# FFN of a decoder block by seven products: sums of products on top of copies in PSUM, last transposes between half pieces, and one weight-block sum by accumulating DMA

## The chip, the cores and the metric

The kernel runs on one core of one Trainium2 chip. The metric is the device time of one execution in microseconds, lower is better; the median of several executions is what two kernels are compared by. Beside the time there is one profiled execution, from which all rows below are read.

## What is computed

The reference is a whole decoder block for 512 tokens of width 2048 in float32: two attention branches merged by gates, then a SwiGLU FFN with 5632 hidden columns. The change touches the FFN alone:

```python
h2 = _rms(x, g_norm2) * (1 + sc2) + sh2
gate, up = jnp.split(h2 @ w_ffn_in, 2, axis=-1)
x = x + gt2 * ((jax.nn.silu(gate) * up) @ w_ffn_out)
```

Here `sh2`, `sc2` and `gt2` are vectors of 2048 that are computed from a conditioning vector.

## The kernel before

**The products.** Each of the two FFN matrix products is cut into 2 x 2 blocks and done with seven block products in place of eight (Strassen's scheme in Winograd's form). The blocks of a weight matrix are called 11, 21, 12, 22; the blocks of the activations are 11, 12, 22 and the sums "1" to "4" (S1 to S4). `PROD` says what each product multiplies: P1 takes weight block 11, P5 the difference 12 - 11, P7 the difference of 22 and that, P3 block 22, P6 the difference of 22 and 11, P2 block 21, P4 the difference of 21 and 22's running sum. So four of the seven products (P5, P7, P6, P4) need a sum of two weight blocks, made by VectorE (DVE) in the buffer of one of them (`piece_make`; `INTO` names that buffer and `LAST` says which buffers a product frees).

**A piece.** Every float32 product is done in three passes with a high and a low part of each operand (`mm3`). A weight piece is a tile of 128 x 1024, 512 KB: loaded by SP's DMA queue into one of ten buffers `raw`, cast to its high part `whi` by ScalarE (ACT), the rest `wlo` made by DVE, then used by 12 TensorE matmuls of 128 x 512. There are three `whi` and three `wlo` buffers. `ahead_to(i, 2, 6)` sets the order: before piece i is used, pieces up to i+2 are made and up to i+6 are loaded. All engines run their instructions in the order in which this walk emits them, each engine its own list.

**Stage a** (`ffn_in_group`, `w_ffn_in`) has 11 groups of hidden columns; each product of a group is four pieces. The first four groups are "early": their P1 and P2 are made ahead in one stretch (32 pieces) and parked in DRAM, so their group loop has P5, P7, P3, P6, P4 only. The others run P1, P5, P7, P3, P6, P2, P4. Products accumulate in four pairs of PSUM banks: A (tags s, s), B (t, t), C (mm, mm), D (mm, y). Partial results that several outputs share are evacuated and added by DVE (`p1`, `z`, `u`, `c12`; tiles of 128 x 512); after P4 a silu and a product by `z` follow. `act_back1` and `act_back2` transpose the two hidden halves back on TensorE (4 transposes into a bank of tag mm, 4 into one of tag y), split them into high and low parts and park them in DRAM by GpSimd's (POOL) queue; `act_back2` also makes the sums S1 to S4. `act_back2` of a group runs in the next group: after P1, or in early groups after P5. That of group 10 runs behind P1 of stage b.

**Stage b** (`ffn_out_chunk`, `w_ffn_out`) goes through five chunks of groups and the two halves q = 0 and 1 of the output columns; parked activations (`yb`) come back by SP's queue. After each product DVE adds its bank to an accumulator `acc`; in the final chunk `finish` combines them after P6, and `out_tiles` transposes the results on TensorE, adds them to the residual `xo` by DVE and stores them. The end of the program is the final chunk for q = 0 and then for q = 1, in the order P1, P5, P7, P3, P6, P2, P4.

In the rows, line L83 is that of a helper which records every operation, so tiles are told apart by names; L179 issues SP's DMAs, L1370 and L1400 the parks, L1545 the stores of the output.

Of the kernel before, what the change touches and what calls it, by code (L numbers as in the profile page):

```python
# [88 lines left out]
def kernel(  # L89
# [943 lines left out]

    def half_cols(th):
        return slice(th * 256, th * 256 + 256)
# [36 lines left out]
    X = {}  # L1072

    def norm2(k, th):
# [6 lines left out]
        if name != (2, 1):  # L1081
# [3 lines left out]
            X[name, k % 8] = x[:, 0:256], x[:, 256:512]  # L1085
        act.activation(t, t, AF.Identity, bias=sh)

    def sums(a, b, put):
# [7 lines left out]
        vec.tensor_tensor(s34[:, hi], b[:, lo], s12[:, hi], ALU.subtract)  # L1096
# [42 lines left out]
    BLOCK = {"11": (0, 0), "21": (1, 0), "12": (0, 1), "22": (1, 1)}  # L1139
# [21 lines left out]

    def kmc(key, ap):
# [12 lines left out]
    INTO = {"P5": "11", "P7": "12", "P6": "22", "P4": "21"}  # L1175
    LAST = {"P7": ("12",), "P6": ("11",), "P4": ("21", "22"), "E1": ("11",), "E2": ("21",)}

    def piece_keys(stage, g, prod, j):
        _, x, y = PROD[prod]
        return [(stage, g, b, j) for b in (y, x) if b]  # L1180

    def piece_make(stage, g, prod, j):
        _, x, y = PROD[prod]
        key = (stage, g, x, j)
        if y:
            kd = (stage, g, INTO[prod], j)
            vec.tensor_tensor(raws[kd], raws[key], raws[stage, g, y, j], ALU.subtract)
            key = kd
# [6 lines left out]
        for b in LAST.get(prod, ()):  # L1195
            del raws[stage, g, b, j]
# [4 lines left out]
    cur = {"load": 0, "make": 0}  # L1201
# [6 lines left out]
    def add_do(fn):  # L1208
        ev.append((None, fn))

    def ahead_to(i, n_make, n_load):
        while cur["load"] < min(i + n_load + 1, len(pieces)) or cur["make"] < min(i + n_make + 1, len(pieces)):
# [4 lines left out]
            else:  # L1217
                made[cur["make"]] = piece_make(*pieces[cur["make"]])
# [13 lines left out]
    def prod_mm(bank, hl, w, kk, first, last):  # L1232
# [3 lines left out]
        xh, xl = hl  # L1236
# [31 lines left out]
    def ffn_in_group(g, early):  # L1268
# [21 lines left out]
        def copy_to(name, bank):  # L1290
            def fn(t):
                G[name, t] = t2(name)
                act.copy(G[name, t], G[bank][t])
            both(fn)

        def add_bank(name, bank, out=None):
            def fn(t):
                dst = G[name, t] if out is None else t2(out)
                vec.tensor_tensor(dst, G[name, t], G[bank][t], ALU.add)
                G[out or name, t] = dst  # L1300
            both(fn)

        def after_p6(t):
            u, z = G["u", t], G["z", t]
            vec.tensor_tensor(z, z, u, ALU.add)
# [342 lines left out]
```

## Time and profile before

| | us |
|---|---|
| median of 3 runs | 2665.55 |
| lowest and highest | 2661.05, 2666.24 |
| profiled execution | 2668.23 |
| its span, first to last instruction | 2666.5 |
| stage a, ahead part and groups, about | 1308 to 2203 |
| stage b | 2203 to 2663 |

The profile lists the busy time of the engines: PE is TensorE's matmul, PEld its weight loads, DVE VectorE, ACT ScalarE, POOL GpSimd, SP the engine that issues most DMAs. A view by windows gives the same for stretches of the span, together with the granted TensorE clock (1.00 is full) and the share of the 16 DMA engines' time that is used. A view of waits names, for the idle time of an engine, what ended it.

### The profile page before, as it was taken

What the parts mean: (1) busy time and instruction counts of PE and PEld (TensorE: products, weight loads), DVE (VectorE), ACT (ScalarE), POOL (GpSimd) and SP (SyncE); (2) the same over time, 40 slices, a digit from 0 to 9 for tenths busy, and PEclk for the clock granted to TensorE, in tenths of its full rate; (3) what the DMA queues carried; (4) which work ended last, traced back from release to release, by engine and by line L of the source; (5) the groups of instructions that cost most, each with busy time, mean ns of one, the idle gap of its engine ahead of it and who ended that gap; (6) DMA issues with size and microseconds to landing.
All of it is one profiled execution on the core that took longest, in us unless ns stands there. A gap on an engine that the chain in (4) does not pass through costs nothing.

```text
span 2666.5 us, 32303 instructions
## 1 busy us (share of the span) xinstructions
PE 2582.4 (97%) x12166; PEld 2145.6 (80%) x12166; DVE 2023.5 (76%) x2622; ACT 1147.9 (43%) x1557; POOL 162.9 (6%) x270
## 2 busy tenths in 40 slices
PE   6999999999999999999899999999999999999998
PEld 4788888888998888888787777888878787888876
DVE  8967766656788764633688999888888887789997
ACT  4434655542333322322474545445554445533332
POOL 0000000000100100000000111011110011000000
PEclk9999999999999999999999999999999999999998
DMA  8854444336667694343575665554544459676561
GB/s 343 295 204 153 159 151 138 136 117 255 237 253 259 240 352 166 133 151 118 147 223 162 213 216 186 165 162 132 174 153 126 160 169 318 203 235 207 188 214 41
DMA packets 260901, 510.37 MB, mean 191 GB/s; under 512 B 16453, under 2 KB 181061, under 8 KB 235657
## 3 DMA queue, kind: packets, MB, share of 16 engines
q1 hardware_dynamic: 239136, 447.01, 49.4%
q0 software_dynamic: 15552, 50.61, 5.2%
q10 hardware_dynamic: 6056, 10.70, 1.1%
q8 instruction: 95, 1.56, 0.2%
q14 instruction: 62, 0.50, 0.1%
HBM read 445.86 MB, written 62.39 MB: 191 GB/s over the span
## 4 chain that ended last, share of the span: by engine, by line
PE 74%; issue 15%; DVE 6%; DMA 3%; POOL 1%; ACT 1%; SPq 0%; POOLq 0%; ACTq 0%; DVEq 0%
PE ps_mm L83 47%; PE ps_s L83 11%; PE ps_t L83 10%; PE ps_y L83 5%; DVE wlo L83 2%; DMA raw<-in_w_ff_dram 1%; DVE raw L272 1%; POOL apark L1370 1%; ACT whi L83 1%; DVE acc L83 1%; DVE raw L83 1%; DMA gpark<-sg 0%; DMA raw<-in_w_ada_dram 0%; DVE s L83 0%; DMA apark<-y34h 0%
## 5 line engine op out<-in xcount | busy, mean ns | idle before, releaser
L83 ACT CAST whi<-raw 128x1024 fp32r<-128x1024 f32 x672 | 703.0, 1050 | 1023.8 <-PE ps_mm L83 456.6
L83 DVE TENSOR_TENSOR wlo<-raw,whi 128x1024 fp32r<-128x1024 f32 x672 | 816.3, 1219 | 315.8 <-ACT whi L83 305.3
L83 DVE TENSOR_TENSOR raw<-raw,raw 128x1024 f32<-128x1024 f32 x264 | 319.1, 1221 | 28.0 <-DMA raw<-in_w_ff_dram 25.4
L83 PE MATMUL ps_mm<-hl,whi 128*128 128x512 f32 x832 | 327.6, 394 | 0.0
L83 PE MATMUL ps_mm<-hh,whi 128*128 128x512 f32 x832 | 325.5, 391 | 0.0
L83 PE MATMUL ps_mm<-hh,wlo 128*128 128x512 f32 x832 | 325.3, 391 | 0.0
L272 DVE CUSTOM_DVE_ANT_0 raw<-raw,cb,cols 128x2048 f32<-128x2048 f32 x96 | 224.6, 2345 | 1.0 <-DMA raw<-in_w_ada_dram 1.0
L83 PEld LDWEIGHTS ps_mm<-hh,wlo 128*128 128x128 f32 x832 | 156.5, 188 | 32.7
L83 PEld LDWEIGHTS ps_mm<-hh,whi 128*128 128x128 f32 x832 | 156.7, 188 | 30.7
L83 PEld LDWEIGHTS ps_mm<-hl,whi 128*128 128x128 f32 x832 | 157.0, 189 | 30.4
L83 PE MATMUL ps_s<-whi,x 128*128 128x512 f32 x576 | 179.2, 393 | 0.0
L83 PE MATMUL ps_mm<-whi,yb 128*128 128x512 f32 x440 | 138.9, 397 | 0.0
L83 PEld LDWEIGHTS ps_s<-whi,x 128*128 128x128 f32 x576 | 109.3, 190 | 22.8 <-DVE x L83 0.2
L83 PE MATMUL ps_s<-wlo,x 128*128 128x512 f32 x288 | 114.4, 397 | 3.9 <-DVE wlo L83 2.1
L83 PE MATMUL ps_s<-whi,yb 128*128 128x512 f32 x352 | 109.7, 393 | 0.0
L83 PE MATMUL ps_mm<-whi,x 128*128 128x512 f32 x352 | 108.4, 389 | 0.0
L83 PE MATMUL ps_t<-whi,yb 128*128 128x512 f32 x352 | 108.4, 389 | 0.0
L83 PE MATMUL ps_mm<-mgl,whi 128*128 128x512 f32 (+1 forms) x272 | 102.7, 377 | 0.0
L83 PE MATMUL ps_mm<-mgh,whi 128*128 128x512 f32 (+1 forms) x272 | 102.4, 377 | 0.0
L83 PE MATMUL ps_mm<-mgh,wlo 128*128 128x512 f32 (+1 forms) x272 | 102.4, 377 | 0.0
L83 PEld LDWEIGHTS ps_mm<-whi,yb 128*128 128x128 f32 x440 | 85.2, 194 | 18.0
L83 PE MATMUL ps_mm<-wlo,yb 128*128 128x512 f32 x220 | 88.3, 401 | 5.7 <-DVE wlo L83 5.7
(378 smaller groups left out, 5221.9 us busy)
## 6 DMA issues: line engine op xcount, KB each, us to landing
raw<-in_w_ff_dram SPq DMA_DIRECT2D x296, 512.0 KB, 5.1
raw<-in_w_ada_dram SPq DMA_DIRECT2D x96, 1024.0 KB, 5.1
yb<-apark SPq DMA_DIRECT2D x154, 256.0 KB, 5.5
raw<-in_w_gate_dram SPq DMA_DIRECT2D x27, 1024.0 KB, 4.9
raw<-in_w_sb_dram SPq DMA_DIRECT2D x24, 1024.0 KB, 5.3
raw<-in_w_out_dram SPq DMA_DIRECT2D x16, 1024.0 KB, 4.8
raw<-in_w_gate_dram SPq DMA_DIRECT2D x24, 512.0 KB, 4.7
raw<-in_w_lat_dram SPq DMA_DIRECT2D x8, 1024.0 KB, 8.1
```

The source lines that it names most:

```text
L83: ins = f(*a, **kw)
L272: tc.keep_in_program_order(nc.vector.tensor_tensor_reduce(raw, raw, cb, 1.0, col(C_B + 16 * ADA[name] + j), ALU.mult, ALU.add, dst))
L1370: nc.gpsimd.dma_start(pk(i, a, 2, part), t.bitcast(F32).rearrange("p (a x) -> p a x", a=2))
```

## The change

The signs of some activation blocks' sums are turned, so that all four weight sums become additions. In stage a, P6 now precedes P3 and P7, and its sum is made in block 11's buffer; P4 uses that running sum.

**T3 by DMA.** The third weight sum, that of P7, is not made on DVE. Block 12 is loaded a second time into a `raw` buffer of its own (`T3`) by SP's queue, and POOL's queue adds block 22 onto it by a DMA with `accum_op`, issued four pieces ahead of the piece being made (`raw_add`, `cur["add"]`). That makes 66 more loads and 66 accumulating DMAs of 512 KB each (44 in stage a, 22 in stage b), and 66 DVE sums fewer (264 to 198).

**Sums of products in PSUM.** In stage a, bank pair D begins as an ACT copy of P1 and P6 accumulates on it; C begins as an ACT copy of D, and P7, then P4, accumulate on C. DVE adds `u += B` after P3 and `z += C` after P7, and the silu after P4 reads C itself. For each group DVE has 8 operations of 128 x 512 for 14, ACT 12 for 8. Four extra matmuls (`mark_banks`) write the banks of tags mm and y once at the start of stage a.

**act_back2** makes both halves' sums first, then all casts, and in early groups stands in front of P5, directly behind the `act_back1` of the group before.

**The last transposes** (`out_tile`) of the final chunk stand between half pieces of P2 and P4 (6 matmuls each) in banks s, t, y, and no longer between P2 and P4 as one run. A negated `gt2` (`ngt2`) serves the output columns whose sign is turned.

```diff
     def sums(a, b, put):
...
-        vec.tensor_tensor(s12[:, lo], a[:, hi], b[:, hi], ALU.add)
-        vec.tensor_tensor(s12[:, hi], s12[:, lo], a[:, lo], ALU.subtract)
+        vec.tensor_tensor(s12[:, lo], b[:, hi], a[:, hi], ALU.subtract)
+        vec.scalar_tensor_tensor(s12[:, hi], s12[:, lo], -1.0, a[:, lo], ALU.mult, ALU.subtract)
...
+    def raw_add(key, onto):
+        src, km = raw_src(key)
+        nc.gpsimd.dma_start(raws[onto].rearrange("p (a b) -> p a b", b=128 if km else 256), src,
+                            accum_op=ALU.add)
...
-        "P1": ((1, 1), "11", None), "P5": (1, "12", "11"), "P7": (3, "22", "12"), "P3": (4, "22", None),
+        "P1": ((1, 1), "11", None), "P5": (1, "12", "11"), "P7": (3, "T3", None), "P3": (4, "22", None),
...
+    INTO = {"a": {"P5": "11", "P6": "11", "P4": "21"}, "b": {"P5": "11", "P6": "22", "P4": "21"}}
...
+    def piece_add(stage, g, prod, j):
+        if prod == "P7":
+            raw_add((stage, g, "22", j), (stage, g, "T3", j))
...
             else:
+                while cur["add"] < min(cur["make"] + 4, cur["load"]):
+                    piece_add(*pieces[cur["add"]])
+                    cur["add"] += 1
                 made[cur["make"]] = piece_make(*pieces[cur["make"]])
                 cur["make"] += 1
...
+        def before_d(t):
+            if t == 0:
+                G["D"] = tb("mm", "y")
+            act.copy(G["D"][t], G["p1", t] if early else G["A"][t])
...
         def after_p6(t):
+            if t == 0:
+                G["C"] = tb("mm", "mm")
+            act.copy(G["C"][t], G["D"][t])
+            G["u", t] = t2("u")
+            act.copy(G["u", t], G["D"][t])
+
+        def after_p3(t):
+            u = G["u", t]
+            vec.tensor_tensor(u, u, G["B"][t], ALU.add)
+
+        def after_p7(t):
+            z = G["z", t]
+            vec.tensor_tensor(z, z, G["C"][t], ALU.add)
...
         def after_p4(t):
-            u = G["u", t]
-            vec.tensor_tensor(u, u, G["C"][t], ALU.add)
-            act.activation(u, u, AF.Silu)
-            vec.tensor_tensor(u, u, G["z", t], ALU.mult)
+            s = t2("silu2")
+            act.activation(s, G["C"][t], AF.Silu)
+            vec.tensor_tensor(s, s, G.pop(("z", t)), ALU.mult)
...
-        if g > 0 and not early:
+        if g > 0:
             add_do(lambda: act_back2(g - 1))
+        both(before_d)
         product("P5", "B", True, False)
-        copy_to("z", "B")
-        if g > 0 and early:
-            add_do(lambda: act_back2(g - 1))
-        product("P7", "C", True, False)
-        add_bank("z", "C")
-        product("P3", "B", False, True)
-        product("P6", "D", True, True)
+        both(after_p5)
+        product("P6", "D", False, True)
+        both(after_p6)
+        product("P3", "B", False, True)
+        both(after_p3)
+        product("P7", "C", False, False)
+        both(after_p7)
...
+    def mark_banks():
+        for o in tb("mm", "mm", "mm", "y"):
+            pe.matmul(o, onesr, X[(1, 1), 0][2], start=True, stop=True)
...
                     for kk in range(2):
+                        if final and prod == "P2" and gi + kk > 0:
+                            out_tile(q, 1, 2 * gi + kk - 1, (0, 1), ("y", "t", "t")[2 * gi + kk - 1])
+                        if final and prod == "P4":
+                            if gi == kk == 0:
+                                out_tile(q, 1, 3, (0, 1), "y")
+                            else:
+                                out_tile(q, 0, 2 * gi + kk - 1, (0,), ("t", "t", "y")[2 * gi + kk - 1])
+                                if gi == kk == 1:
+                                    out_tile(q, 0, 3, (0,), "t")
...
-            if final and prod == "P2":
-                add_do(lambda: out_tiles(q, 1, (0, 1)))
-                add_do(lambda: out_tiles(q, 0, (0,)))
             if final and prod == "P4":
-                add_do(lambda: out_tiles(q, 0, (1,)))
+                for i in range(4):
+                    add_do(lambda i=i: out_tile(q, 0, i, (1,), ("s", "t", "s", "t")[i]))
```

What this does to the order of instructions is seen at three places. The first is TensorE at the border of the early groups 1 and 2. Before: behind P4 (last row with `x_`) stand the transposes of `act_back1` (out of `s_`), then P5 (`ps_t`), and behind P5 the transposes of `act_back2` of the group before (out of `p_`); the bracket says which engine's semaphore an instruction waits for.

```order
L83 MATMUL ps_mm_12234<-whi_12491,x_11564 128x512 x2
...
L83 MATMUL ps_mm_12550<-consts,s_2210_12458 128x128 [waits DVE_49]
...
L83 MATMUL ps_t_12587<-wlo_12510,x12h_11005 128x512 [waits DVE_49]
...
L83 MATMUL ps_t_12588<-whi_12604,x12l_11573 128x512
L83 MATMUL ps_mm_12658<-consts,p_2138_12088 128x128
```

After, at the same border; `silu_` is here the second hidden half of group 1, made from P4.

```order
L83 MATMUL ps_mm_12324<-whi_12520,x_11574 128x512 x2
L83 MATMUL ps_mm_12580<-consts,s_2224_12488 128x128
...
L83 MATMUL ps_y_12593<-consts,s_2225_12490 128x128
L83 MATMUL ps_mm_12610<-consts,silu_2240_12574 128x128 [waits DVE_49]
L83 MATMUL ps_mm_12610<-consts,silu_2241_12577 128x128 [waits DVE_49]
...
L83 MATMUL ps_y_12627<-consts,silu_2240_12574 128x128 [waits Activation_49]
...
L83 MATMUL ps_t_12679<-wlo_12540,x12h_11015 128x512
```

The transposes out of P4's own result have moved from behind P5, 48 matmuls later, to directly behind P4 and `act_back1`.

The second place is TensorE in the final chunk for q = 1, behind P6. Before: the end of P2 (`ps_s`), the 24 transposes out of `acc_` in groups of four or two, then P4 (`ps_mm` out of `wlo_`).

```order
L83 MATMUL ps_s_21040<-whi_21213,yb_20622 128x512 x2
L83 MATMUL ps_mm_21284<-consts,acc_18672 128x128 [waits DVE_49]
...
L83 MATMUL ps_y_21291<-consts,acc_18672 128x128
...
L83 MATMUL ps_mm_21298<-consts,acc_18672 128x128 [waits DVE_49]
...
L83 MATMUL ps_y_21327<-consts,acc_18803 128x128 [waits DVE_49]
...
L83 MATMUL ps_mm_21124<-wlo_21250,yb_20662 128x512
```

After, the same place from the start of P2 on:

```order
L83 MATMUL ps_s_21175<-wlo_21331,yb_20744 128x512 [waits DVE_49]
...
L83 MATMUL ps_s_21176<-whi_21330,yb_20744 128x512 x2
L83 MATMUL ps_y_21395<-consts,acc_18776 128x128 [waits DVE_49]
...
L83 MATMUL ps_s_21175<-wlo_21331,yb_20746 128x512
...
L83 MATMUL ps_t_21413<-consts,acc_18776 128x128
...
L83 MATMUL ps_y_21441<-consts,acc_18776 128x128 [waits DVE_49]
...
L83 MATMUL ps_mm_21260<-wlo_21386,yb_20791 128x512
```

The first four transposes now stand behind 6 matmuls of P2 in place of 24, and the rest alternates with half pieces.

The third place is POOL's list where stage b begins. After: behind the parks of `act_back1` of group 10 (`y1h`, `y1l`) stand three accumulating DMAs (L1173), and behind them the parks of `act_back2`. In the list of before these parks follow each other directly.

```order
L1396 DMA apark_349<-y1h_17954 128x2x256 [waits DMASW0_49,Activation_49]
L1396 DMA apark_349<-y1l_17955 128x2x256 [waits DMASW1_49,DVE_49]
L1173 DMA raw_3282_17972<-in_w_ff_dram 128x4x256 [waits DMAHW6_49,DMAHW0_49,DMASW2_49]
L1173 DMA raw_3287_17992<-in_w_ff_dram 128x4x256 [waits DMAHW7_49,DMAHW1_49,DMASW3_49]
L1173 DMA raw_3290_18012<-in_w_ff_dram 128x4x256 [waits DMAHW0_49,DMASW4_49]
L1437 DMA apark_348<-x_3297_18043 128x512 [waits DMASW5_49,DVE_49]
```

An accumulating DMA waits for the SP load of its own buffer (`DMAHW`) and for POOL's earlier DMAs on its semaphore (`DMASW`), and what follows in POOL's list waits behind it.

## Rows read from the trace of the kernel before

**Rows 1.** The page, part 1: busy time, share of the span, instructions.

```profile
PE 2582.4 (97%) x12166; PEld 2145.6 (80%) x12166; DVE 2023.5 (76%) x2622; ACT 1147.9 (43%) x1557; POOL 162.9 (6%) x270
```

**Rows 2.** Windows: stretch, length, busy PE, PEld, DVE, ACT, POOL; clock, DMA share, GB/s.

```profile
1395.00:1620.00 225.00, 215.12 (x956) 173.94 (x955) 205.04 (x237) 110.44 (x135) 31.27 (x46) 1.00 0.63 200
1620.00:2203.00 583.00, 573.45 (x2575) 471.77 (x2574) 491.07 (x543) 286.17 (x345) 67.89 (x98) 1.00 0.49 158
2203.00:2235.00 32.00, 26.28 (x114) 21.38 (x113) 25.36 (x34) 17.83 (x27) 9.69 (x14) 0.89 0.98 353
2235.00:2581.00 346.00, 346.00 (x1529) 286.48 (x1528) 294.36 (x294) 146.76 (x151) 0.00 (x0) 1.00 0.66 217
2581.00:2608.30 27.30, 20.34 (x84) 15.35 (x83) 23.70 (x34) 5.14 (x5) 4.98 (x10) 0.81 0.39 135
...
2636.80:2663.00 26.20, 19.63 (x82) 14.64 (x80) 18.38 (x29) 2.10 (x2) 2.16 (x4) 0.80 0.18 66
```

**Rows 3.** Waits of PE, 1395 to 1620: total us, times, longest us.

```profile
PE ps_t L83 <- DVE wlo L83: 5.4, 6, 1.5
PE ps_mm L83 <- DVE wlo L83: 3.6, 5, 1.3
```

**Rows 4.** Waits of PE, 1620 to 2203.

```profile
PE ps_mm L83 <- DVE wlo L83: 8.8, 8, 1.8
```

**Rows 5.** Waits of PE, 2203 to 2667.

```profile
PE ps_mm L83 <- DVE xo L83: 9.9, 3, 4.7
```

**Rows 6.** PE's timeline after one wait: start, us, instruction, idle before.

```profile
1407.31 0.50 PE L83 MATMUL ps_t<-wlo,x12h 128*128 128x512 f32 x1 [0.87 <-ACT s L83]
1407.65 0.40 PE L83 MATMUL ps_t<-whi,x12h 128*128 128x512 f32 x1
```

**Rows 7.** Groups of DVE, 1395 to 2203: count, busy us, mean ns, idle before.

```profile
L83 DVE TENSOR_TENSOR wlo<-raw,whi 128x1024 fp32r<-128x1024 f32 x281 | 341.2, 1222 | 81.6 <-ACT whi L83 80.4
L83 DVE TENSOR_TENSOR raw<-raw,raw 128x1024 f32<-128x1024 f32 x175 | 210.5, 1221 | 23.2 <-DMA raw<-in_w_ff_dram 22.3
```

**Rows 8.** Group of ACT in the same stretch.

```profile
L83 ACT COPY z<-ps_t 128x512 f32<-128x512 f32 x22 | 12.2, 586 | 7.2 <-PE ps_t L83 6.8
```

**Rows 9.** Timeline behind the last P4 of stage a, DVE and ACT.

```profile
2201.83 1.28 DVE L83 TENSOR_TENSOR p<-p,ps_mm 128x512 f32<-128x512 f32 x2
...
2203.27 1.15 ACT L83 ACTIVATE p<-p 128x512 f32<-128x512 f32 x2
...
2205.45 0.58 ACT L83 COPY y<-ps_y 128x512 f32<-128x512 f32 x1
```

**Rows 10.** Timeline of the longest wait between the stages.

```profile
2223.79 1.99 ACT L83 CAST whi<-raw 128x1024 fp32r<-128x1024 f32 x2
...
2226.14 0.79 PE L83 MATMUL ps_mm<-wlo,yb 128*128 128x512 f32 x1 [5.72 <-DVE wlo L83]
```

**Rows 11.** Windows behind two stalls of PE, columns as in rows 2.

```profile
2226.10:2232.00 5.90, 5.86 (x19) 4.73 (x20) 2.54 (x3) 2.64 (x4) 0.00 (x0) 0.71 0.88 270
...
2648.00:2656.00 8.00, 7.53 (x24) 5.54 (x25) 4.06 (x8) 0.00 (x0) 2.16 (x4) 0.50 0.48 176
```

**Rows 12.** Timeline of the end, q = 1.

```profile
2636.66 0.68 DVE L83 TENSOR_TENSOR acc<-acc,ps_mm 128x512 f32<-128x512 f32 x1
...
2637.85 4.90 DVE L83 TENSOR_TENSOR acc<-acc,acc 128x512 f32<-128x512 f32 x8
...
2642.39 0.60 PE L83 MATMUL ps_mm<-consts,acc 128*128 128x128 f32 x4
...
2642.82 0.60 PE L83 MATMUL ps_y<-consts,acc 128*128 128x128 f32 x4
...
2648.15 1.12 PE L83 MATMUL ps_mm<-consts,acc 128*128 128x128 f32 x4 [4.73 <-DVE xo L83]
```

**Rows 13.** DMA issues, 1300 to 2203: KB each, median us to landing.

```profile
raw<-in_w_ff_dram SPq DMA_DIRECT2D x206, 512.0 KB, 5.1
```

**Rows 14.** DMA issues, 2203 to 2667.

```profile
apark<-y1l POOLq DMA_DIRECT2D x2, 256.0 KB, 6.1
```

More of the change, by code (lines that the diff above doesn't have):

```diff
@@ L1072, with minus_gt2 @@
     X = {}
+    ngt2 = cp.tile([P, KD], F32, name="ngt2")
+    def minus_gt2():
+        vec.tensor_scalar(ngt2, ada["gt2"], -1.0, None, ALU.mult)
+    step(minus_gt2)
     def norm2(k, th):
@@ L1084, in norm2 @@
             vec.scalar_tensor_tensor(x[:, 256:512], t, sh, x[:, 0:256].bitcast(F32), ALU.add, ALU.subtract)
-            X[name, k % 8] = x[:, 0:256], x[:, 256:512]
+            X[name, k % 8] = x[:, 0:256], x[:, 256:512], x
         act.activation(t, t, AF.Identity, bias=sh)
@@ L1184, in piece_make @@
         key = (stage, g, x, j)
+        if prod == "P4":
+            y = T2_AT[stage]
         if y:
-            kd = (stage, g, INTO[prod], j)
-            vec.tensor_tensor(raws[kd], raws[key], raws[stage, g, y, j], ALU.subtract)
+            kd = (stage, g, INTO[stage][prod], j)
+            vec.tensor_tensor(raws[kd], raws[key], raws[stage, g, y, j], ALU.add)
             key = kd
@@ L1194, in piece_make @@
         vec.tensor_tensor(v4(lo), kmc(key, r), v4(hi).bitcast(F32), ALU.subtract)
-        for b in LAST.get(prod, ()):
+        for b in LAST[stage].get(prod, ()):
             del raws[stage, g, b, j]
@@ L1200 @@
     made = {}
-    cur = {"load": 0, "make": 0}
+    cur = {"load": 0, "add": 0, "make": 0}
     pieces = []
@@ L1288, in both, with after_p5 @@
             add_do(lambda: [fn(t) for t in range(2)])
[L1290 to L1301, printed above, removed]
-        def after_p6(t):
-            u, z = G["u", t], G["z", t]
-            vec.tensor_tensor(z, z, u, ALU.add)
-            c12 = t2("c12")
-            vec.tensor_tensor(c12, u, G["B"][t], ALU.add)
-            G["c12", t] = c12
+        def before_d(t):
+            if t == 0:
+                G["D"] = tb("mm", "y")
+            act.copy(G["D"][t], G["p1", t] if early else G["A"][t])
+            if early:
+                del G["p1", t]
+        def after_p5(t):
+            G["z", t] = t2("z")
+            act.copy(G["z", t], G["B"][t])
+        def after_p6(t):
+            if t == 0:
[9 more added lines that the diff above has]
+            vec.tensor_tensor(z, z, G["C"][t], ALU.add)
         def after_p2(t):
@@ L1376, in back @@
                 c = j + 2 * b
-                pe.transpose(o[:, b * 256 + t * P:b * 256 + (t + 1) * P], src[t][:, c * P:(c + 1) * P], ident)
+                pe.matmul(o[:, b * 256 + t * P:b * 256 + (t + 1) * P], src[t][:, c * P:(c + 1) * P], ident,
+                          start=b == t == 0, stop=b == t == 1, is_transpose=True, skip_group_check=True)
     def act_back1(g):
@@ L1432, in second_norms @@
         x_sums(k)
+    at_product(4, mark_banks)
     at_product(1, lambda: last_sum(1))
@@ L1532, in out_load, with out_tile @@
             sync_dma(xres[m], xpark[m])
[L1534 to L1545 removed]
+    def out_tile(q, col_, i, rows, tag):
+        m = 4 * (2 * q + col_) + i
+        o = ps(tag)
+        for r in rows:
+            for t in range(2):
+                pe.transpose(o[:, (2 * r + t) * P:(2 * r + t + 1) * P],
+                             fin[q, r + 1, col_ + 1, t][:, i * P:(i + 1) * P], ident)
+        xr = xres[m]
+        cs = slice(256 * rows[0], 256 * rows[-1] + 256)
+        vec.scalar_tensor_tensor(xr[:, cs], o[:, cs], (ngt2 if col_ == 0 else ada["gt2"])[:, m:m + 1], xr[:, cs], ALU.mult, ALU.add)
+        (nc.gpsimd if q == 0 or rows[-1] == 0 else nc.sync).dma_start(outT[m * P:(m + 1) * P, cs], xr[:, cs])
     for ci in range(len(CH)):
```

59 lines of the change are left out of this document (23 added, 36 removed).

## The prediction

> **What bounds the kernel now.** The page's busy times come first: TensorE is busy for 97% of the span, DVE 76%, ACT 43% [rows 1]. So the time can only fall where TensorE waits, or where its clock is low. The windows say where that is [rows 2]. In the main part of stage b (2235 to 2581) TensorE is busy for 346.00 of 346.00 us at clock 1.00: nothing is to be had there, whatever DVE is spared. In stage a it lacks 9.9 us of the early groups' 225 and 9.6 of the other groups' 583. Around the border of the stages it lacks 5.7 of 32 at clock 0.89, and in the two tails (q = 0 and q = 1) 7.0 of 27.3 and 6.6 of 26.2 at clocks 0.81 and 0.80. The waits name the causes: in stage a `wlo` from DVE (5.4 and 3.6 us in the early groups, 8.8 in the others) [rows 3, 4], in the tails `xo` from DVE, 9.9 [rows 5]. DVE is busy for 91% of the early groups and 84% of the others [rows 2], so there it is late because it is full. Sums of weight blocks take 210.5 us of it [rows 7].
>
> **Stage a, the gain.** The waits are 5.4 + 3.6 + 8.8, and 0.7 that the windows hold beside them, 18.5 us over some 20 stops. A matmul that starts after a stop takes 0.34 us to the next in place of 346.00 / 1529 = 0.226 [rows 6, 2], so each stop costs 0.11 more: 20.7 in all. The change takes from each group four sums of 1.22 [rows 7] and six operations of 0.68 [rows 12], 9.0 us. In the early groups DVE falls from 205 by 36 to 169 of 225 us (75%), in the seven others from 491 by 63 to 428 of 583 (73%). I take it that most stops go; waits of three stops at the mean of 1 us and their restarts stay, 3.4. Gain 17.3.
>
> **Stage a, what is new.** (1) At the three borders between early groups the transposes out of P4's own result stand directly behind P4. TensorE does the 8 transposes of `act_back1` (0.43 for four [rows 12], 0.9), then waits for ACT: two silus 1.15 [rows 9], a copy, a cast and a copy, each about 0.59 [rows 8, 9], which free the bank of tag y. With the last four transposes and 0.15 of signalling TensorE goes on 1.15 + 1.8 + 0.45 + 0.35 = 3.75 us after P4, where 16 transposes without a wait are 1.75: 2.0 more, three times 6.0. Queued behind this on PE is P5, whose pieces are made, so all of it is lost. (2) In early groups P4 follows P7 directly on bank pair C, and its first write waits until DVE has read C for `z`: half of one operation of 0.68, 0.35 in each of four groups, 1.4. (3) `mark_banks` is four matmuls of 0.226, 0.9. (4) ACT has four more copies a group: 44 x 0.59 = 26 us, beside 110 + 286 busy of 808: ACT goes from 49% to 52%, which TensorE's work hides. Together 8.3, and stage a gains 9.0.
>
> **T3.** The loads and accumulating DMAs add 44 x 2 of 512 KB to stage a, where the DMA engines are used to 0.63 and 0.49 [rows 2]. Nothing in this trace accumulates, so its landing time L is bounded by rows: from below by a load of the same size, 5.1 [rows 13]; from above by two parks of half the size at the busiest place, 2 x 6.1 = 12.2 [rows 14], times 1.5 because the old value is read besides, 18.3. The room is this: T3 of P7's third and fourth piece gets the buffer that P3's first and second leave, eight pieces before its use. Eight pieces of 12 matmuls are 21.7 us; 5.1 for the load and 1.05 + 1.22 for cast and `wlo` leave some 14. I take L near the load, 5 to 9, so the cost is 0, hidden by the matmuls of P3 and P7; it is 11 x (L - 14) where that cover is too thin. Behind an accumulating DMA in POOL's list stand parks, which it holds back by a load's 5.1 us; the parks' readers come in stage b, so that costs nothing but at the border.
>
> **Border of the stages.** TensorE waits 5.72 for the `wlo` of a piece, since ACT's casts come in turn with DVE's sums of `act_back2` and `whi` is cast only at 2223.79 [rows 10]. Behind it the clock is 0.71 for 5.9 us, which costs 5.9 x 0.29 = 1.7 [rows 11]; with the restart 7.5. With all sums first the alternation is gone. Left over: 1.5, because DMA is used to 0.98 there [rows 2] and three accumulating DMAs stand ahead of the parks. Gain 6.0.
>
> **The tails.** Before, each tail runs P2, 8 transposes, a wait of 4.7, 16 transposes at low clock (0.50 over 8 us, 4.0 lost [rows 11]), P4 and the last transposes. From the end of P6 it takes 27.1 us (q = 0, up to the next P1) and 26.2 (q = 1, up to the last `xo`). The wait is DVE's: two additions out of the banks and eight of 4.90 in all after P6 [rows 12]. After the change the first transposes need the ninth of these ten, 0.6 + 0.68 + 7 x 0.61 = 5.5 us after P6, and stand behind only 6 matmuls of P2 (1.36): TensorE waits 4.2 earlier than it did, but nothing in DVE's chain is shorter. What is won lies behind it: half pieces cover the `xo` operations (0.75 each). At full clock: 48 matmuls 10.9, 24 transposes 2.6, the wait 4.2, so P4 ends at 17.7; then 1.7 up to the next P1 for q = 0 (19.4) and 2.7 for the last operations at q = 1 (20.4). That gains 7.7 + 5.8 = 13.5. But a wait of 4.73 is followed by clock 0.50, waits of at most 1.8 in stage a by none below 1.00 [rows 2, 4, 11]; 4.2 is nearest to 4.73. So I charge a low clock, between the 1.7 and the 4.0 of rows 11 and nearer to the second: 3.3 a tail. Gain 6.9; the ends are 13.5 and, with 4.0 and 1.0 of further waits for `xo`, 3.5.
>
> **Sum.** 9.0 + 6.0 + 6.9 = 21.9 us less. On the profiled execution, 2668.2 with a span of 2666.5, that makes 2646.3; it lies 2.7 above the median 2665.55, so for the median 2643.6. Its own range, from the ends above (stage a 4 to 16, border 3 to 7.5, tails 3.5 to 13.5, hardly all at one end): 2632 to 2653.
>
> **A page against this change.** The rows say 0.98 of DMA at the border and 0.63 in the early groups. The Trainium skill, "DMA: Bandwidth & Descriptors", section "Issuing engines are not separate DMA queues", says that DMAs of SP and GpSimd run on the same 16 engines and interleave; by that T3's second load and its accumulation lengthen SP's loads too. No row shows it yet. Its section "Anatomy of one DMA" gives about 2.0 us + bytes / 436e3, which would be an estimate of 3.2 us for 512 KB; this trace has 5.1, and the measurement decides. By the page's figure the rival of a late T3 would lose its chance; by the rows it keeps it.
>
> **Rivals.** *T3 lands late (slower).* Place: P7's third piece in each group of stage a, where ACT's cast waits for the accumulation, and DVE's `wlo` and all later pieces with it. For it: no such DMA in the trace, an upper bound of L of 18.3, and DVE idles 22.3 us for loads even now [rows 7], so the buffers are tight. Against: 14 us of room and a DMA share of half. Price at the upper bound 11 x 4.3 = 47: 2665.6 - 21.9 + 47 = 2691. It turns the sign from L = 14 + 21.9 / 11 = 16.0.
>
> *The stops stay (no change).* DVE idles 81.6 us before `wlo`, and 80.4 of that is ended by ACT's `whi` [rows 7]. If the stops come from ACT's place in the chain and from loads and not from DVE's load, fewer sums bring nothing: the 17.3 go, the new 8.3 stay, and border and tails give 12.9, in all 4.6 us: 2661. Against it is that DVE is busy for 91% where the stops are densest. This is also where it lands if T3 saves DVE work that was hidden.
>
> *More falls away.* The wait in the tails is short enough to keep the clock (6.6 more), the borders of the early groups overlap (6.0), and neither stops nor border leave a rest (4.9): 39.4 less, 2626. For it: 4.2 is less than any stall whose low clock rows 11 show. Against: it needs several things at once.
>
> **How the numbers follow.** Forecast 0.57, more 0.15, stops stay 0.15, late T3 0.13. Predicted is the likeliest, 2643.6. The range leaves out most of the late T3 and the far end of the better case: 2623 to 2664. About 0.2% of 2665.55, 5.3 us, is what a measurement of this kernel can tell from no change. Faster (under 2660.2): 0.57 + 0.15, and 0.07 of the case that centres on 2661: 0.79. Same: 0.08 of that case and 0.01 of a T3 slightly late: 0.09. Slower: 0.12, nearly all of the late T3.
>
> **What the profile after would show.** Stage a right: PE's waits for `wlo` in the groups down to some 3 us, three waits for ACT or DVE of about 2 at the early borders; DVE busy for about 75%. T3 right: no wait of PE or ACT that ends with an accumulating DMA, its landing under 14 us. Border: the wait of 5.7 gone. Tails: one wait of about 4.2 behind the first half piece of P2, some 19 to 24 us from P6's end to the end in place of 27.1 and 26.2. Wrong: a cast of T3 that waits for POOL's queue; waits for `wlo` that move to P6 or P4 and keep their sum; a clock under 1.00 inside stage a, or a clock of 1.00 through the tails.

## The result: slower by 1.0%, and where the time lies in the profile after

The changed kernel takes 2691.1 us (median, 2690.9 to 2692.1), the kernel before 2664.3 in the same comparison: a ratio of 1.0103, with a 95% interval of 1.0085 to 1.0120. The forecast was 2643.6 with a range up to 2664; the sign was wrong. The profiled execution took 2691.2, its span is 2689.5.

The page's first part shows what the change did to the engines; it answers to [rows 1].

```profile
PE 2593.3 (96%) x12170; PEld 2156.6 (80%) x12170; DVE 1917.9 (71%) x2491; ACT 1172.0 (44%) x1609; POOL 248.7 (9%) x336
```

DVE has 106 us less to do, as intended, and TensorE is busy for 11 us more with four more instructions: part of its work ran at a low clock. To see where, the span is cut at points that both kernels have: the first transposes of `act_back1` of group 3 (1642.9 before, 1689.4 after) and of group 10 (2202.1, 2235.0), and the end of P6 in either tail. Windows of the kernel before (stretch, length, busy PE, PEld, DVE, ACT, POOL; clock, DMA share, GB/s):

```profile
1395.00:1642.90 247.90, 238.02 (x1057) 192.84 (x1056) 225.97 (x259) 118.88 (x143) 31.27 (x46) 1.00 0.65 206
1642.90:2202.10 559.20, 549.65 (x2465) 451.99 (x2464) 469.24 (x520) 277.05 (x336) 67.89 (x98) 1.00 0.48 153
2202.10:2581.40 379.30, 373.58 (x1649) 309.08 (x1648) 321.02 (x329) 165.27 (x178) 9.69 (x14) 0.99 0.69 228
```

and of the changed kernel, with its two tails in the last rows:

```profile
1395.00:1689.40 294.40, 253.85 (x1049) 203.74 (x1048) 196.80 (x219) 127.85 (x165) 53.19 (x62) 0.93 0.81 226
1689.40:2235.00 545.60, 545.60 (x2466) 453.06 (x2464) 416.66 (x449) 291.27 (x365) 105.08 (x126) 1.00 0.75 213
2235.00:2614.10 379.10, 374.42 (x1649) 308.94 (x1648) 297.57 (x307) 164.53 (x178) 36.47 (x36) 1.00 0.92 280
2614.10:2635.80 21.70, 17.10 (x82) 13.04 (x81) 19.97 (x30) 4.56 (x5) 4.39 (x8) 0.92 0.73 241
2663.20:2686.20 23.00, 18.16 (x81) 13.81 (x79) 18.00 (x29) 2.10 (x2) 2.16 (x4) 0.85 0.19 74
```

| stretch | before | after | difference |
|---|---|---|---|
| four early groups | 247.9 | 294.4 | +46.5 |
| seven other groups | 559.2 | 545.6 | -13.6 |
| border and stage b up to P6 of the first tail | 379.3 | 379.1 | -0.2 |
| tails, q = 0 and q = 1 [rows 2] | 27.1 + 26.2 | 21.7 + 23.0 | -8.6 |

So the other groups and the tails gained what was forecast or more, the border of the stages gained nothing, and the early groups lost all of it and 23 us more. In the seven other groups TensorE is busy for 545.60 of 545.60 us: not one wait is left. In the early groups it idles for 40.6 us in place of 9.9, and about as many instructions take 15.8 us longer, at a mean clock of 0.93.

TensorE's waits in the early groups (total us, times, longest), the answer to [rows 3]:

```profile
PE ps_mm L83 <- DVE wlo L83: 15.0, 4, 5.2
PE ps_t L83 <- DVE wlo L83: 12.2, 3, 4.4
PE ps_mm L83 <- DVE z L83: 9.1, 4, 4.0
PE ps_mm L83 <- DVE silu L83: 3.1, 6, 0.9
```

The first row is one stop in P7 of each group, the second one in P5 behind each border, the third one before P4. What ACT and DVE wait for in the same stretch says what stands behind them. ACT:

```profile
ACT y L83 <- DMA apark<-y1h: 18.9, 3, 6.8
ACT whi L83 <- DMA raw<-in_w_ff_dram: 15.3, 4, 4.0
```

DVE:

```profile
DVE raw L83 <- DMA raw<-in_w_ff_dram: 30.5, 11, 4.5
```

ACT waits three times for a park of `y1h` to land, and four times for a T3; DVE waits 30.5 us for weight loads before its sums. The stop in P7 of group 1 shows how the last of these reaches TensorE, first DVE, then TensorE (start, us, instruction, idle before):

```profile
1514.19 1.23 DVE L83 TENSOR_TENSOR raw<-raw,raw 128x1024 f32<-128x1024 f32 x1 [2.23 <-DMA raw<-in_w_ff_dram]
1515.33 1.22 DVE L83 TENSOR_TENSOR wlo<-raw,whi 128x1024 fp32r<-128x1024 f32 x1
1516.60 0.79 PE L83 MATMUL ps_mm<-wlo,x34h 128*128 128x512 f32 x1 [2.96 <-DVE wlo L83]
```

A sum for P4 waits for its load, and the `wlo` of P7's second piece stands behind that sum in DVE's list. ACT's wait for T3 ends only at 1516.02 and is for a later piece. Here is the first of the three borders, first POOL, then ACT, then TensorE:

```profile
1470.13 0.74 POOL L1396 DMA_DIRECT2D apark<-y1h  x1 [38.01 <-ACT y1h L83]
...
1478.67 0.58 ACT L83 COPY y<-ps_y 128x512 f32<-128x512 f32 x1 [6.77 <-DMA apark<-y1h]
...
1483.55 0.80 PE L83 MATMUL ps_t<-wlo,x12h 128*128 128x512 f32 x1 [4.34 <-DVE wlo L83]
```

ACT's copy of the last `y` gets the buffer of a `y1h` tile whose park was issued 8.5 us before, and all casts of `whi` queue behind that copy. What is different beside the park is seen in SP's list, first after the change, then before (in the kernel before, the park of `y1h` stands at 1466.71):

```profile
1468.96 2.13 SPq L179 DMA_DIRECT2D raw<-in_w_ff_dram  x4
```

```profile
1472.47 2.44 SPq L179 DMA_DIRECT2D raw<-in_w_ff_dram  x2
...
apark<-y1h POOLq DMA_DIRECT2D x6, 256.0 KB, 2.6
```

After the change four weight loads are issued directly before and beside the park; before it, none is until the park has landed, in 2.6 us (the last line, from the DMA view of 1395 to 1640: median to landing). And the DMA view of the early groups (1395 to 1660: queue, packets, MB, share of 16 engines; then issues with median us to landing):

```profile
q1 hardware_dynamic: 43560, 38.57, 47.1%
q0 software_dynamic: 13648, 19.93, 32.5%
...
raw<-in_w_ff_dram SPq DMA_DIRECT2D x68, 512.0 KB, 6.3
raw<-in_w_ff_dram POOLq DMA_DIRECT2D x16, 512.0 KB, 7.6
...
apark<-y1h POOLq DMA_DIRECT2D x6, 256.0 KB, 8.3
```

The accumulating DMAs are the second `raw` row. Their median of 7.6 us is inside the 5 to 9 that the prediction took. The last one of each group, for which ACT's cast waits, took 10.6 to 11.5.

### The profile page after: what moved, and what is told of

It is laid out like the page before. It is cut to its first block, busy times and chain, and to the rows that moved or that the text cites. A ratio compares the mean times of both kernels' runs of the same rounds, so it can differ in the third digit from the quotient of the medians.

```text
span 2689.5 us, 32627 instructions
## 1 busy us (share of the span) xinstructions
PE 2593.3 (96%) x12170; PEld 2156.6 (80%) x12170; DVE 1917.9 (71%) x2491; ACT 1172.0 (44%) x1609; POOL 248.7 (9%) x336
## 4 chain that ended last, share of the span: by engine, by line
PE 83%; issue 7%; DMA 4%; DVE 4%; ACT 1%; POOL 0%; ACTq 0%; DVEq 0%; POOLq 0%; SPq 0%
PE ps_mm L83 52%; PE ps_s L83 13%; PE ps_t L83 13%; PE ps_y L83 5%; DMA raw<-in_w_ff_dram 2%; DVE wlo L83 1%; DVE raw L272 1%; DMA apark<-y1h 1%; ACT whi L83 1%; DVE acc L83 0%; DMA gpark<-sg 0%; ACT sq L83 0%; DMA raw<-in_w_ada_dram 0%; DMA s<-epark 0%; POOL apark L1396 0%
## 5 line engine op out<-in xcount | busy, mean ns | idle before, releaser
L83 DVE TENSOR_TENSOR raw<-raw,raw 128x1024 f32<-128x1024 f32 x198 | 241.5, 1221 | 35.4 <-DMA raw<-in_w_ff_dram 32.0
L1173 POOL DMA_DIRECT2D raw<-in_w_ff_dram x66 | 86.5, 1336 | 504.8 <-DMA raw<-in_w_ff_dram 157.2
L868 POOL TENSOR_SCALAR_AFFINE_SELECT sa<-sa 128x128 f32<-128x128 f32 x32 | 17.3, 540 | 871.5 <-ACT sa L83 871.5
```

The source lines that it names most:

```text
L83: ins = f(*a, **kw)
L868: nc.gpsimd.affine_select(a[:, dg], a[:, dg], pattern=[[-1, P]], compare_op=ALU.is_gt, fill=0.0, base=0, channel_multiplier=1)
L1173: nc.gpsimd.dma_start(raws[onto].rearrange("p (a b) -> p a b", b=128 if km else 256), src, accum_op=ALU.add)
```

## The experiments

Times below are medians of each run; the kernel before lay at 2663 to 2664 in all of them. Group intervals are read from the trace, between the first transposes of `act_back1`.

**act_back2 of the early groups behind the third piece of P5** (theory A).

```diff
-        if g > 0:
-            add_do(lambda: act_back2(g - 1))
-        both(before_d)
+        if not early:
+            add_do(lambda: act_back2(g - 1))
+            both(before_d)
...
                 add_piece(("a", g, prod, j), lambda w, j=j: use(w, j))
+                if prod == "P5" and early and j == 2:
+                    if g > 0:
+                        add_do(lambda: act_back2(g - 1))
+                    both(before_d)
```

> The changed kernel with one thing moved: in the early groups act_back2 (and the copies of P1 into bank pair D) stands behind the third piece of P5, no longer directly behind act_back1. Theory A (border): after P4, ACT's copy of the last y tile waits about 6.8 us because it gets the buffer of a y1h tile whose park was just issued and lands 8 us later; this stops TensorE for 4 us at three borders and lowers its clock behind. By A these stops go and the time is about 2668 (3 x (4.1 + 1.1 + about 2.5 of low clock) = 23 less than 2691). Theory B (sums): what costs is that DVE's list has the sums for P4, which wait for block 21's load, ahead of P7's wlo; by B alone the time stays at 2686 to 2691. Theory C (accumulation): the accumulating DMAs load the DMA engines so that everything lands late; by C the stop only moves, 2683 to 2691.

Measured 2674.9, 16.2 less than the changed kernel (ratio to before 1.0041, 1.0024 to 1.0057). The copies of P1 into bank pair D (`before_d`) moved with it. In the early groups' waits the border's stops for `wlo` are gone (three of at most 1.9 us for ACT's copies into D are left), and the other two are almost unchanged:

```profile
PE ps_mm L83 <- DVE wlo L83: 15.2, 6, 4.7
PE ps_mm L83 <- DVE z L83: 10.4, 4, 5.4
```

So the border is a real part, 16 us, and not the whole.

**Early groups as before the change** (order P5, P7, P3, P6, P4, T3 by DVE, sums on SBUF); the rest as changed.

```diff
+        if early:
+            product("P5", "B", True, False)
+            both(o_z)
+            if g > 0:
+                add_do(lambda: act_back2(g - 1))
+            product("P7", "C", True, False)
...
```

> The changed kernel with the four early groups of stage a run as before the change: products in the order P5, P7, P3, P6, P4, T3 summed by DVE in block 12's buffer, sums of products on SBUF, act_back2 behind P5. The other seven groups, stage b, the border and the tails as changed. If the whole loss lies in the early groups (there the trace shows 46.5 us more than before from the first to the fourth group's end, and 13.6 + 9.9 less in the rest) the time is about 2645. If the loss comes from accumulating DMAs wherever they are, only some 16 of 66 go and the time stays above 2675.

2656.5, ratio 0.9969 (0.9956 to 0.9982), 34.6 less: the loss lies in the early groups, which take 248.7 us here. The gain is less than the 46 expected, mainly since the first group after them takes 84.5 us in place of 78.0. In three of the early groups P7 has a stop of 2.9 to 3.1 behind `act_back2`.

**No accumulating DMAs at all** (theory C).

```diff
-        if prod == "P7":
+        if prod == "P7" and stage == "none":
             raw_add((stage, g, "22", j), (stage, g, "T3", j))
```

> The changed kernel without the 66 accumulating DMAs (T3 is then block 12 alone, so the products P7 are not what the reference asks; the second load of block 12 stays). Theory C (accumulation): with 34 MB less moved and parks no longer sharing a queue with it, loads and parks land as before the change and the time falls to 2645 to 2655. Theories A and B (place and order): the stops at the borders and at P7 stay, somewhat shorter, since act_back2's place and DVE's list are the same: 2675 to 2688.

2666.3, 24.8 less. The early groups take 276.2 us, 18.2 less, the seven others the same, and from there to the end it is 5.9 less:

```profile
1395.00:1671.20 276.20, 246.74 (x1045) 199.48 (x1044) 195.87 (x217) 127.38 (x165) 31.06 (x46) 0.95 0.64 209
1671.20:2217.30 546.10, 546.10 (x2466) 453.05 (x2465) 417.24 (x449) 291.66 (x365) 67.56 (x98) 1.00 0.57 186
```

Neither expectation held alone: the accumulations cost 25 us. Without them P7's stops are gone and those at the borders (3.3 to 5.5 us) stay. The park of `y1h` lands late with and without them (8.3 and 7.9 us), so it is not the accumulations that delay it. In the runs of this case, parks of `y1h` in stage a that had four or five weight loads issued beside them took 6.7 to 9.9 us, and those with none 2.4 to 2.9.

**DVE's sums and `wlo` of stage a in the order of the code** (theory B, first form).

```diff
-            vec.tensor_tensor(raws[kd], raws[key], raws[stage, g, y, j], ALU.add)
+            i_ = vec.tensor_tensor(raws[kd], raws[key], raws[stage, g, y, j], ALU.add)
+            if stage == "a":
+                tc.keep_in_program_order(i_)
```

> The changed kernel with DVE's sums of weight blocks and its wlo in stage a kept in the order in which the code emits them, so that P7's wlo of a piece no longer stand behind the sums for P4, which wait for block 21's load. Theory B (sums): the stops of 5.2, 3.0 and 3.6 us at P7, those of 1.1 to 4.0 for z at P4 and the low clock behind them go: about 16 to 20 less, 2671 to 2675. Theory A alone: 2687 to 2691. If keeping the order costs something of its own (sums that were made early are made late), 2691 to 2700.

2815.7, far beyond any expectation. DVE's timeline of this run in a group where nothing else is short:

```profile
1750.13 1.22 DVE L83 TENSOR_TENSOR raw<-raw,raw 128x1024 f32<-128x1024 f32 x1
1752.52 1.23 DVE L83 TENSOR_TENSOR wlo<-raw,whi 128x1024 fp32r<-128x1024 f32 x1 [1.17 <-ACT whi L83]
1753.66 1.22 DVE L83 TENSOR_TENSOR raw<-raw,raw 128x1024 f32<-128x1024 f32 x1
```

A sum, ACT's cast, then `wlo`, one piece after the other, take 1753.66 - 1750.13 = 3.5 us where TensorE needs a piece every 2.7. So DVE's list is not the order of the walk, as was said of all engines in the description of the kernel: where no order is kept, the framework's scheduler sets it, and its habit of making a sum one piece early is what hides the cast. The run tells nothing of theory B, because it changed too much.

**Only P7's `wlo`, P4's sums and `z` kept in order, in early groups** (theory B, second form).

```diff
+            if stage == "a" and g < NPRE and prod == "P4":
+                tc.keep_in_program_order(i_)
...
+        if stage == "a" and g < NPRE and prod == "P7":
+            tc.keep_in_program_order(i_)
```

> The changed kernel with one order kept on DVE in the four early groups only: wlo of P7's pieces, then the sums for P4's first two pieces, then the additions of z, then the sums for P4's last two; everything else is free as before. Theory B (in DVE's list the sums for P4, which wait for block 21's load, hold up P7's wlo and z): the stops of 5.2, 3.0, 3.6 and 3.3 us at P7 and of 1.1 to 4.0 for z go with their low clock, 15 to 20 less than the changed kernel: 2671 to 2676. Theory D (it is T3 itself that lands late, ACT's cast of it waits for the accumulation, and the list only hides that): the stops stay at the same pieces, 2686 to 2692.

2690.2, no change. The early groups' waits show that P7's stops went and those before P4 grew by as much:

```profile
PE ps_mm L83 <- DVE z L83: 19.5, 4, 8.5
PE ps_t L83 <- DVE wlo L83: 13.9, 3, 5.0
PE ps_mm L83 <- DVE wlo L83: 4.5, 5, 1.6
```

Theory B falls as a cause of the lost time, and so does D as it was put: T3's own landing is not what P7 must wait for, since with the list turned P7 ran, though ACT still waited 11.9 us for T3. DVE's list decides where the lateness shows; the lateness is that of the loads.

**That order together with act_back2 behind P5** (the edits of two runs above, nothing else).

> The last kernel and the one with act_back2 behind the third piece of P5 put together. If border (16 us by its own run) and DVE's list are two separate costs, the gains add: 2655 to 2662. If both only shift the same lateness of loads and accumulations, the sum is much less than the parts: 2670 to 2676.

2684.7, outside both ranges: 5.5 less than the order alone and 9.8 more than the place alone. The kept order costs something and buys nothing.

**T3 of stage a summed by DVE on the second load of block 12.**

```diff
         if prod == "P7":
-            raw_add((stage, g, "22", j), (stage, g, "T3", j))
+            if stage == "a":
+                r = raws[stage, g, "T3", j]
+                vec.tensor_tensor(r, r, raws[stage, g, "22", j], ALU.add)
+            else:
+                raw_add((stage, g, "22", j), (stage, g, "T3", j))
...
```

The part left out lets the pieces of P7 in stage a be loaded and summed one piece earlier.

> The changed kernel with T3 in stage a summed by DVE again (onto the second load of block 12, which stays), so 44 accumulating DMAs go and 44 DVE sums of 1.22 us come back; stage b as changed. Theory C' (accumulations cost in the early groups, and sparing DVE these sums buys nothing in the other seven): early groups as in the run without accumulations (17 us less), the seven others stay at 78.0 us a group: 2672 to 2676. Rival (the relief of DVE is what took the stops out of the seven groups): these go back to 79 to 80 us, 7 to 14 more, 2680 to 2690.

2678.7, 12.4 less, between the two ranges. Its windows show both signs:

```profile
1395.00:1668.80 273.80, 245.27 (x1046) 198.50 (x1045) 213.87 (x233) 127.62 (x165) 31.07 (x46) 0.96 0.64 212
1668.80:2221.20 552.40, 548.38 (x2465) 452.21 (x2464) 447.91 (x477) 292.53 (x365) 67.56 (x98) 1.00 0.56 184
```

Early groups 20.6 less than the changed kernel, the others 6.8 more. So accumulating T3 by DMA buys 1 us a group in the seven (DMA share 0.75 with it) and costs 5 us a group in the early ones (0.81). Its DMA view of 1395 to 1660, beside that of the changed kernel above:

```profile
q1 hardware_dynamic: 48845, 44.24, 53.0%
q0 software_dynamic: 3680, 12.06, 11.3%
...
raw<-in_w_ff_dram SPq DMA_DIRECT2D x78, 512.0 KB, 5.1
...
apark<-y1h POOLq DMA_DIRECT2D x6, 256.0 KB, 8.4
```

Without the accumulations POOL's queue takes 11.3% of 265 us in place of 32.5%: 56.2 us less, and 7.87 MB less, which is 15 of the 16 (the last one's data move after the window). That is 3.7 us of all 16 engines for each accumulating DMA of 512 KB. The loads take 53.0% for 44.24 MB, 1.66 us for 512 KB. An accumulation costs rather more than two loads. The park of `y1h` takes 8.4 us here too, at a DMA share of 0.64.

**Early groups as before, and T3 of stage b by DVE into block 12.**

```diff
-            "b": {"P5": ("12",), "P7": ("T3",), "P6": ("11",), "P4": ("21", "22")}}
+            "b": {"P7": ("12",), "P6": ("11",), "P4": ("21", "22")}}
```

> The kernel with early groups as before the change, and in stage b T3 summed by DVE into block 12 (no second load, no accumulation there); the seven other groups of stage a and the tails as changed. If the accumulations at the border are what keeps a stop of 2.9 and 1.4 us there (the run without any gained 5.9 from the end of stage a on), 2649 to 2652; if the stop there is DVE's own work, 2655 to 2658 as without this edit.

2649.0, ratio 0.9947 (0.9932 to 0.9962), 7.5 less than with accumulations in stage b. The border's longest stop, in the changed kernel and here:

```profile
2256.70 0.50 PE L83 MATMUL ps_mm<-wlo,yb 128*128 128x512 f32 x1 [2.85 <-DVE wlo L83]
```

```profile
2215.58 0.50 PE L83 MATMUL ps_t<-wlo,yb 128*128 128x512 f32 x1 [1.04 <-DVE wlo L83]
```

So T3 by DMA in stage b is what ate the border's gain; the run without any accumulation, which keeps the second loads, has no stop there at all. Whether it is the place of the accumulations ahead of the parks or their DMA time, no run separates.

**Eleven raw buffers, 67 other tiles** (theory E).

```diff
-    tp = ctx.enter_context(tc.tile_pool(name="tp", bufs=68))
+    tp = ctx.enter_context(tc.tile_pool(name="tp", bufs=67))
...
-        st["rp2"] = ctx.enter_context(tc.tile_pool(name="rp2", bufs=10, reuse_waits="tile"))
+        st["rp2"] = ctx.enter_context(tc.tile_pool(name="rp2", bufs=11, reuse_waits="tile"))
```

> The changed kernel with eleven raw buffers in place of ten (and 67 tiles of 2 KB in place of 68 for everything else). Theory E (each T3 holds a buffer through a load, a wait in POOL's list and an accumulation, so block 21's loads start too late in the early groups): one buffer more lets each of those loads start about one piece, 2.7 us, earlier: the stops of 3 to 5 us at P7 and for z shrink by about that in each early group, 8 to 16 less with the low clock behind them, 2675 to 2683. Theory F (the 16 DMA engines are what is short there, at a share of 0.80): no gain, 2688 to 2693. With a tile less the wait of ACT's y copy at the borders stays in both.

2688.9, with single runs from 2685.7 to 2697.9: no clear change. P7's stops went (15.0 to 2.3 us in all), those at the border grew (12.2 to 20.3), so the tile that was taken away spoiled the test. It was repeated without the border, and with a control.

**Eleven raw buffers with act_back2 behind P5, and the same with ten.**

> Eleven raw buffers and 67 other tiles, with act_back2 of the early groups behind the third piece of P5, so that a tile less costs nothing at the border. Theory E (T3 holds a raw buffer through load and accumulation, and block 21's loads start late for want of a buffer): the stops at P7 go as in the run with eleven buffers, and now show in the time, 10 to 15 less than the 2675 of that place of act_back2 with ten: 2660 to 2665. Theory F (engine time of the accumulations, buffers are no limit): 2673 to 2677.

> The same with ten raw buffers and 67 other tiles: the control for the tile that is taken away. Both theories: 2674 to 2680, the time of that place of act_back2 with 68 tiles or a few us more; what lies between this run and the last is the eleventh buffer alone.

2682.4 with eleven, 2675.8 with ten: the eleventh buffer costs 6.7 us. TensorE's waits with eleven and with ten, in this order:

```profile
PE ps_t L83 <- DVE wlo L83: 13.0, 3, 4.7
PE ps_mm L83 <- DVE z L83: 9.5, 4, 4.3
...
PE ps_mm L83 <- DVE wlo L83: 3.9, 4, 1.0
```

```profile
PE ps_mm L83 <- DVE wlo L83: 17.0, 7, 4.7
PE ps_mm L83 <- DVE z L83: 6.9, 4, 3.8
```

The stops move from P7 to P3 and about keep their sum, and DVE waits 31.4 us for loads with eleven, 27.0 with ten. With eleven buffers the loads land later (median 6.9 us against 6.3 with ten), so buffers are not what is short. Theory E falls. F stands, though its range for eleven (2673 to 2677) was missed too, with this sum behind it: in the changed kernel the DMA engines are busy for 0.81 x 294.4 = 238 us in the early groups, and the matmuls of that stretch take 238 at full clock (the row of before). Before, it was 0.65 x 247.9 = 161. A high share alone is not it: from the border to the first tail it is 0.92 after the change, and TensorE idles for only 4.7 of 379.1 us there. That the accumulations cost is shown by the two runs without them; that they do so by engine time, and not by their turn in POOL's list, is argued from this sum.

**Both gains together: T3 of stage a by DVE, act_back2 behind P5** (the two edits above).

> The two edits that gained alone, together: T3 of stage a summed by DVE on the second load of block 12 (12 us by its run) and act_back2 of the early groups behind the third piece of P5 (16 us by its run). If accumulation and border are separate causes, the gains add: 2661 to 2666. If the park of y1h is slow because of the accumulations, so that the border's cost goes with them, only the larger gain is left: 2672 to 2677. If moving act_back2 only helps by giving the accumulations time, the time stays at 2677 to 2680.

2660.1, 31.0 less (16.2 + 12.4 = 28.6): the gains add, so they are separate causes. The early groups take 254.3 us here, 40.1 of the 46.5 are accounted for. The other 6.4 stay open; the trace shows a stop of 2.0 to 3.4 us for `z` in each early group. The kernels whose early groups run in the former order have none, so it comes with P4 directly behind P7 on one bank pair.

**A version that beats both.** The kernel of 2649.0, with the inner order of `act_back2` as before the change (casts in turn with sums) in the four early groups.

```diff
+            if g < NPRE:
+                park(2 * g + j, 3, split_t(s12, "y12"))
...
+            if g < NPRE:
+                park(2 * g + j, 5, split_t(s34, "y34"))
+                continue
```

> The kernel of 2649 (early groups as before the change, T3 by DVE there and in stage b) with act_back2 of the four early groups in its former inner order, casts in turn with sums. Where the early groups' transposes come behind P5, the new order (all sums first) leaves stops of 2.8 to 5.9 us for wlo in the trace; if that order is the cause there, they fall to the 1.3 to 1.5 us of before and the time to 2639 to 2643. If the stops come from DVE's load alone, 2647 to 2650.

2640.9, ratio 0.9917 (0.9902 to 0.9932). Its windows, early groups and others:

```profile
1395.00:1641.50 246.50, 238.22 (x1058) 193.26 (x1057) 226.31 (x259) 119.14 (x144) 31.17 (x46) 1.00 0.64 208
1641.50:2191.50 550.00, 546.94 (x2465) 452.81 (x2464) 418.77 (x452) 291.93 (x365) 104.87 (x126) 1.00 0.74 212
```

All sums first costs 8.1 us for the four early groups, where DVE is 92% busy: in the trace of 2649.0, ten short operations (3.4 us) in a row stand ahead of the next `wlo`. Whether it helps elsewhere, no run tells.

**The same with P6 on a copy of P1 in the early groups.**

```diff
         def o_u(t):
-            vec.tensor_tensor(G["p1", t], G["p1", t], G["D"][t], ALU.add)
             G["u", t] = G.pop(("p1", t))
+            act.copy(G["u", t], G["D"][t])
...
-            product("P6", "D", True, True)
+            product("P6", "D", False, True)
```

> The same, with P6 of the early groups accumulating on an ACT copy of P1 in bank pair D, so that DVE has two operations of 0.68 us less in each early group. If DVE's load sets their remaining stops, 3 to 6 less than that kernel: 2634 to 2640; if not, the same as it.

2642.7 (2634.8 to 2644.6): no difference that can be told from the last. Two DVE operations less for each early group buy nothing that shows.

## Why the prediction was wrong, point by point

**Stage a, the gain: right for seven groups.** The stops for `wlo` were DVE's load, and with that lighter they went, all of them: 13.6 us against the 10 or so that the steps give for these groups. T3's part of it is 6.8 (the run with T3 by DVE), so the rest, about 7, is that of the sums in PSUM and the other edits, which no run separates.

**T3: the step that failed.** The prediction asked when one accumulating DMA lands. It took 5 to 9 us, the trace has a median of 7.6 in the early groups and 11.5 at most; it found 14 us of room, and called the cost 0, hidden by the matmuls of P3 and P7. Measured, 24.8 us go with the accumulations, 18.2 of them in the early groups. Each T3 of the early groups did land within that room; what came late for P7 were the weight loads beside it. No step asked how much engine time all of them take. From [rows 2], and with the prices measured since, the sum is this: DMA used to 0.63 of the early groups' 225 us is 142; 16 more loads of 1.66 are 27, 16 accumulations of 3.7 are 59, in all 228 of 225. Even at a load's price for an accumulation it would have been 196, without slack for bursts. The rival of a late T3 had the right culprit, but not the mechanism, and that its total (2691) is the measured one is chance: it put a late T3 into all eleven groups, where seven had no stop at all, and the four early ones had stops that followed the loads of block 21, wherever DVE's list put them. Its sign, a cast that waits for POOL's queue, appeared four times, and was not what stopped TensorE.

The rule of the Trainium skill that the prediction weighed here, "DMA: Bandwidth & Descriptors", section "Issuing engines are not separate DMA queues", is borne out: GpSimd's accumulations lengthened SP's loads from 5.1 to 6.3 us in the same stretch. The Trainium skill, same title, section "Rules for kernel authors", says that an accumulating DMA reads its destination and writes it later, and 3.7 us of engine time against 1.66 for a load agrees with such extra traffic.

**Early borders: mis-sized by a wrong dismissal.** The prediction had 2.0 us a border for ACT's chain; that part is there (silu 0.9 and 0.3, `y` 0.2 at the first border, 0.7, 0.3 and 0.4 at the others; 1.4 in all; no row shows the 0.15 of signalling in it). But it also said that late parks cost nothing because their readers come in stage b. A park holds its source tile until it has landed, and ACT's next copy got that very tile: 6.8 us of ACT, 3.5 to 4.4 of TensorE and a low clock behind it, 16 us by its run in place of 6. Before, 11 us of P5 lay between, and the park landed in 2.6 us in place of 8.3, with no burst of weight loads beside it. That burst came with the change too, and no step had it.

**z at P4:** predicted 1.4 in all, measured 9.1 over four stops. `z` stands in DVE's list behind the sums and `wlo` of later pieces; at the longest stop one of these sums had waited 2.9 us for its load. These stops are not the accumulations' doing: without any, they are 12.7 in all.

**Border of the stages:** predicted 6.0, measured 0.2. The old stop of 5.72 went as argued; two new ones (2.9 and 1.4) took its place, and without T3 by DMA in stage b 7.5 came back. The left-over of 1.5 was too small.

**Tails: right.** Forecast 6.9 at a low clock, measured 5.4 + 3.2 = 8.6. The first wait came in two parts with a transpose between:

```profile
2617.59 0.33 PE L83 MATMUL ps_y<-consts,acc 128*128 128x128 f32 x1 [1.93 <-DVE acc L83]
2619.39 0.90 PE L83 MATMUL ps_y<-consts,acc 128*128 128x128 f32 x3 [1.48 <-DVE acc L83]
```

3.4 us in place of 4.2, and a low clock for a shorter time: the tails' clocks are 0.92 and 0.85 where they were 0.81 and 0.80 [rows 2].

**Low clock in the early groups** was in no step: stops of 3 to 5 us there brought 15.8 us more of TensorE time. A stop's price was taken as its length and 0.11 us; here it is about half as much again (15.8 on 30.7 us more of idle time).

## What to carry to other kernels

Work that moves from an engine to DMA has to be costed as time of the DMA engines, summed over each stage at that stage's pace and set against the stage's length; a landing time and a margin for one transfer say nothing on that. An accumulating DMA counts for two loads and more here, so it belongs where a stage's sum leaves room. When a step is moved closer to the one before it, ask which buffers that one's outgoing transfers still hold, not only who reads what they write, and which loads will be issued beside them.

## What the runs showed of the hardware

An accumulating DMA of 512 KB from DRAM onto SBUF took 3.7 us of all 16 DMA engines and landed in 7.6 us (median, early groups), a load of that size 1.66 us and 5.1 to 6.3. In stage a, a park of 256 KB with four or five loads of 512 KB issued beside it took 6.7 to 9.9 us to land, at DMA shares of 0.64 to 0.85 and with or without accumulating DMAs, where it took 2.4 to 2.9 with no load beside it. Eleven raw buffers in place of ten made a kernel 6.7 us slower.
